# Sparse attention on half of the heads while the other half's queries are projected

## The chip, the cores and the metric

One core of a Trainium2 chip runs the whole network in one launch. The engines are TensorE (PE, with its weight loads as PEld), VectorE (DVE), ScalarE (ACT), GpSimd (POOL) and SyncE (SP), which issues the weight loads. The metric is the device time of one execution in microseconds (us), as the median of several runs; a profile is one execution with a trace.

## The reference, cut to what matters

Two networks of two layers run one after the other on 256 tokens of width 1024. The change lies in the second layer of the first, in its sparse attention (NSA). Every head has three branches; with 256 tokens all blocks are selected, and the window covers all tokens, so two of them are causal attention over 256 keys, each with its own keys and values.

```python
def nsa_mixer(h, kv_cmp, kv_slc, kv_win, w_in, w_out):
    proj = h @ w_in                                  # queries of 16 heads, 48 gates
    ...
    s = einsum(qb, k_cmp) - slope * d_cmp            # 15 compressed keys
    p_cmp = masked_softmax(s, d_cmp >= 0)
    ...
    p_sel = masked_softmax(einsum(qb, k_sel) - slope * d_sel, d_sel >= 0)
    p_win = masked_softmax(einsum(qb, kw) - slope * d_win, m_win)
    o = g[0] * (p_cmp @ v_cmp) + g[1] * (p_sel @ v_sel) + g[2] * (p_win @ vw)
    return o @ w_out
```

The second network has, beside the tokens x, a context of 256 tokens, with its own attention and FFN. Nothing in the first network depends on it; the grouped attention (GQA) of the second network's second layer needs its keys and values.

## The kernel before, in words

**Matrices.** All products are made from float32 weights split into a high and a low part: a weight half of 128x1024 (0.5 MB) is loaded by SP into one of 6 `raw` buffers, ACT casts the high part (L246), DVE subtracts it (L247), and PE makes three matmuls where one would do. Two halves are a slab. In the form that projects to transposed outputs (L492 to L494) a half is 24 matmuls of 128x256; in the other form (L510, L511, L514) the matmuls are 128x512. Split halves have 4 buffers. The slab's instructions have a higher priority, so they are placed early. A scheduler in the recording layer may also move instructions of one engine past each other; what stands on an engine is the program's order, which does not change while it runs.

**Vector steps.** The conditioning vectors of all layers are computed beside the main line: a queue of 0.5 MB loads, each with one or two passes of DVE over 128x1024 (L176). `tick`, called once by each slab, gives credit (the phase's rate, 1.38 unless it has its own), and a step is taken when there is enough. `need` takes steps at once until a vector that is wanted is there. It is called at the head of the output projection for the gate row (`grow`) and for the next FFN's scale and shift (`ab`).

**The context stream.** The context's work is a generator in pieces with an estimated price in us. `fd(us)` runs pieces until the price is used up; a price of 1.3 is 12 matmuls. It is called in the attention loop of NSA, at the boundaries between sublayers and in the second network's first attention; in its first FFN (the stage `bffn0`) every fourth slot takes a piece, and the boundary behind it runs all that is left (`fd(1e9)`) before GQA begins.

**NSA** (stage `a11`, function `nsa`). The gates and the four slabs of queries (8 halves, two heads in each) are projected first. Then the compressed branch is computed for all 16 heads and both token tiles (L816 to L832). Then 16 steps follow, 8 head pairs by 2 token tiles: `stage_a` (scores on PE at L857, bias and maximum on DVE at L865 and L867, exponentials on ACT at L869, sums, L873 to L875), `stage_b` (scaling by sum and gate on DVE at L887, transposes, copy), and after both tiles `stage_c` (values at L904 and L908, split at L484 and L485). `stage_a` runs one step ahead of `stage_b`, and each step calls `fd(1.4)` twice, which takes two pieces of 1.3 each time. The output projection (`proj_gen`, 4 slabs) and the boundary with the residual and the next norm come after.

Of the kernel before, what the change touches and what calls it, by code (L numbers as in the profile page):

```python
# [25 lines left out]
TT = T // P  # L26
# [5 lines left out]
NCMP = 15  # L32
# [38 lines left out]
class Slots:  # L71
# [8 lines left out]
    def next(self):  # L80
        self.i += 1
        return self.parts[(self.i - 1) % len(self.parts)]


class Kern:
# [693 lines left out]
    def nsa(self, h, before_last):  # L779
        nc, I = self.nc, self.I  # L780
        qT = self.chunk().rearrange("p (i t) -> p i t", i=8)
        m0, m1 = self.chunk(), self.r1
        dist = m0[:, 0:512].rearrange("p (t s) -> p t s", t=TT)
        nc.sync.dma_start(dist, I["dist"])
        ctab = m0[:, 512:512 + 480].rearrange("p (t a h n) -> p t a h n", t=TT, a=2, h=8)
        nc.sync.dma_start(ctab, I["ctab"])
        pcT = m0[:, 1024:2048].rearrange("p (g t) -> p g t", g=4)
        gates = m1[:, 544:640].rearrange("p (t b a g r) -> p t b a g r", t=TT, b=3, a=2, g=2)
        cscs = Slots(m1[:, 640:896], 256)
        pcs = Slots(m1[:, 1024:2048], 512)  # L790
        pcl = []
        gw = self.raw_half(I["b_gate"])
        ghi, glo = self.split(gw[:, 0:384], 384)
        hhi, hlo = h
        ps = self.ps([48, T])
# [2 lines left out]
                     kt == 0, kt == KT - 1)  # L798
        gt = self.w([P, T], "htmp", bufs=2)[:48]
        nc.scalar.activation(gt, ps, AF.Tanh, scale=0.5)  # L800
        for s in range(4):
            for half, w in enumerate(self.slab(I["b_w_in"][s])):
                ps = self.ps([P, T])
                self.b_tile(ps, h, w)
                nc.scalar.activation(qT[:, 2 * s + half, :], ps, AF.Copy, scale=0.125)
            if s == 0:
                ps = self.ps([P, TT, 48])
                for t in range(TT):
                    nc.tensor.transpose(ps[:, t, :], gt[:, t * P:(t + 1) * P], self.ident[:48, :48])
                nc.vector.tensor_scalar(m1[:, 544:640], ps.rearrange("p t g -> p (t g)"), 0.5, 0.5, op0=ALU.mult,  # L810
                                        op1=ALU.add)
        for t in range(TT):
            sc = cscs.next()[:, 0:240].rearrange("p (h n) -> p h n", h=16)
            ps = self.ps([P, 8, 2, NCMP])
            for i in range(8):
                nc.tensor.matmul(ps[:, i], qT[:, i, t * P:(t + 1) * P],  # L816
                                 self.kcT[:, i // 4].rearrange("p a n -> p (a n)"), start=True, stop=True)
            for par in range(2):
                nc.vector.tensor_tensor(sc[:, 8 * par:8 * par + 8, :], ps[:, :, par, :], ctab[:, t, par], op=ALU.add)
            mx = self.w([P, 16], "cmx", bufs=2)  # L820
            nc.vector.tensor_reduce(mx, sc, axis=AX.X, op=ALU.max)
            nc.vector.tensor_tensor(sc, sc, mx[:, :, None].to_broadcast([P, 16, NCMP]), op=ALU.subtract)
            nc.scalar.activation(sc, sc, AF.Exp)
            sm = self.w([P, 16], "csm", bufs=2)
            nc.vector.tensor_reduce(sm, sc, axis=AX.X, op=ALU.add)
            nc.vector.tensor_scalar(sm, sm, 1e-30, None, op0=ALU.max)
            nc.vector.reciprocal(sm, sm)
            nc.vector.scalar_tensor_tensor(sm, sm, self.col("valid", t, 1), gates[:, t, 0].rearrange(
                "p a b r -> p (a b r)"), op0=ALU.mult, op1=ALU.mult)
            pc = pcs.next().rearrange("p (h s) -> p h s", h=16)  # L830
            nc.vector.memset(pc, 0.0)
            nc.vector.tensor_tensor(pc[:, :, 0:NCMP], sc, sm[:, :, None].to_broadcast([P, 16, NCMP]), op=ALU.mult)  # L832
            pcl.append(pc)

        def cmp_T():
            for t, pc in enumerate(pcl):
                ps = self.ps([P, 4, P])
                for g in range(4):
                    par, gp = g % 2, g // 2
                    s0 = par * 8 + gp * 4  # L840
                    nc.tensor.transpose(ps[:, g, :], pc[:, s0:s0 + 4, :].rearrange("p a b -> p (a b)"), self.ident)
                nc.scalar.copy(pcT[:, :, t * P:(t + 1) * P], ps)

        hid = self.hid8()
        ca, cb = self.chunk(), self.chunk()
        nps = [Slots(ca[:, 0:512], 256), Slots(ca[:, 512:1536], 512)]
        pts = Slots(cb, 768, 2)
        state = {}

        def stage_a(i, t):  # L850
            gp, r = divmod(i, 4)
            nk = (t + 1) * P
            sps = [self.ps([P, 2, T]) for _ in range(2)]
            for br in range(2):
                for par in range(2):
                    hs = slice(64 * par, 64 * par + 64)
                    nc.tensor.matmul(sps[par][:, br, 0:nk], qT[hs, i, t * P:(t + 1) * P],  # L857
                                     self.kT[br][hs, gp, 0:nk], start=True, stop=True)
            res = []
            mx = self.w([P, 2, 2], "nmx", bufs=4)  # L860
            sm = self.w([P, 2, 2], "nsm", bufs=4)
            for par in range(2):
                slope = 2.0 ** (-8.0 * ((2 * gp + par) * 4 + r + 1) / 16.0)
                p = nps[t].next().rearrange("p (b s) -> p b s", b=2)
                nc.vector.scalar_tensor_tensor(p, dist[:, t, None, 0:nk].to_broadcast([P, 2, nk]),  # L865
                                               -slope, sps[par][:, :, 0:nk], op0=ALU.mult, op1=ALU.add)
# [687 lines left out]
```

## Time and profile before

| | |
|---|---|
| median of 3 runs | 2141.49 us (2139.22 to 2143.03) |
| profiled execution | 2140.95 us, its span 2139.2 us |
| PE, DVE, ACT busy | 94%, 76%, 51% of the span |
| mean granted TensorE clock | 0.979 |
| NSA: first matmul of gates and queries | 917.75 us |
| NSA: first matmul of the compressed branch | 950.2 us |
| NSA: first matmul of the output projection | 1107.8 us |
| last matmul of the main line of `bffn0`, first of GQA | 1802.2 us, 1835.0 us |

Times inside the kernel count from the start of the span. Matmuls are pipelined, so a busy PE can still be slow: a dense stretch is told by the number of matmuls in it. Busy time of DVE is the union of its instructions; their durations can overlap a little.

### The profile page before, as it was taken

To read this page: it belongs to the slowest core of one execution; us is meant where nothing else is said; L and a number is where in the kernel's file an instruction comes from. 1 tells how busy PE (TensorE), PEld (TensorE's weight loads), DVE (VectorE), ACT (ScalarE), POOL (GpSimd) and SP (SyncE) were. 2 spreads that over 40 slices of the span, in tenths; PEclk is the share of its full clock that TensorE was granted. 3 is DMA by queue.
4 is the path that set the end of the run, shared out by engine and by line. 5 is a ranking of instruction groups with operands and counts; after the bars stand their busy time and mean duration, and the time that the engine had idled before them with its cause. 6 is when DMAs were issued, how large, how long until landed. Compare 5 with 4: busy or idle time off the path is not lost. (4 is left out here: it accounts for less than half of the span.)

```text
span 2139.2 us, 34672 instructions
## 1 busy us (share of the span) xinstructions
PE 2013.3 (94%) x13158; PEld 1796.2 (84%) x13158; DVE 1625.5 (76%) x2753; ACT 1087.3 (51%) x1769; POOL 133.6 (6%) x188
## 2 busy tenths in 40 slices
PE   6999899999899899899999999999999998989998
PEld 5998797998789788787788989877789997768998
DVE  7878898777877688878978666789888656866554
ACT  4444545443444466656765444547754444555443
POOL 0000201000200000110000000210010001100000
PEclk9999999999999999989999999999999999999999
DMA  8989697988677766544566866554359755414553
GB/s 332 330 309 355 236 327 277 330 292 291 222 258 276 241 230 210 195 157 138 190 238 232 292 221 237 180 207 148 128 207 342 264 191 178 140 53 150 188 186 118
DMA packets 136327, 486.46 MB, mean 227 GB/s; under 512 B 14976, under 2 KB 16480, under 8 KB 135392
## 3 DMA queue, kind: packets, MB, share of 16 engines
q1 hardware_dynamic: 134240, 477.90, 63.7%
q0 software_dynamic: 1728, 6.29, 0.8%
q8 instruction: 103, 1.69, 0.3%
q14 instruction: 64, 0.52, 0.1%
q10 hardware_dynamic: 192, 0.05, 0.0%
HBM read 480.47 MB, written 3.19 MB: 226 GB/s over the span
## 5 line engine op out<-in xcount | busy, mean ns | idle before, releaser
L1049 ACT ACT_TABLE_LOAD x15 | 19.2, 1283 | 6.6 <-DVE dst.diff0.2984_16079 L1047 1.7
L340 ACT ACT_TABLE_LOAD x13 | 16.7, 1283 | 0.2
L273 PE MATMUL ps.a00.6_101<-ident,x 128*128 128x128 f32 x4 | 1.1, 427 | 13.8 <-DMA x<-in_x 13.8
L375 POOL DMA_DIRECT2D G.bffn0.3378_18457<-row.bffn0.3377_18455 x1 | 0.6, 595 | 198.4 <-DMA row.bffn0.3377_18455<-diag.bffn0.3376_18453 198.4
L273 PEld LDWEIGHTS ps.a00.6_101<-ident,x 128*128 128x128 f32 x4 | 0.7, 216 | 13.7 <-issue 13.7
L375 POOL DMA_DIRECT2D G.a02.1032_5643<-row.a02.1031_5641 x1 | 0.6, 595 | 182.2 <-DMA row.a02.1031_5641<-diag.a02.1030_5639 182.2
L734 ACT ACTIVATE chunk.kv.1231_6595<-chunk.kv.1128_6071,cols 128x60 f32<-128x60 f32 x32 | 9.8, 387 | 4.0 <-PE ps.a10.1253_6672 L744 4.0
L375 POOL DMA_DIRECT2D G.a12.2528_13717<-row.a12.2527_13715 x1 | 0.6, 595 | 180.2 <-DMA row.a12.2527_13715<-diag.a12.2526_13713 180.2
L333 ACT ACT_TABLE_LOAD x9 | 11.5, 1283 | 0.2
L375 POOL DMA_DIRECT2D G.bffn2.3890_21467<-row.bffn2.3889_21465 x1 | 0.6, 595 | 171.6 <-DMA row.bffn2.3889_21465<-diag.bffn2.3888_21463 171.6
L401 POOL TENSOR_TENSOR rv.ctx.354_2048<-ss.ctx.352_2044,epsd 128x1 f32<-128x1 f32 x1 | 0.2, 191 | 169.8 <-ACT junk.ctx.351_2043 L394 169.8
L375 POOL DMA_DIRECT2D G.a11.2165_11615<-row.a11.2164_11613 x1 | 0.5, 530 | 116.9 <-DMA row.a11.2164_11613<-diag.a11.2163_11611 116.9
L484 ACT CAST chunk.a01.490_2583<-chunk.a01.492_2585 128x256 fp32r<-128x256 f32 x8 | 3.2, 406 | 8.9 <-DVE chunk.a01.492_2585 L676 8.9
L287 PE MATMUL ps.a00.38_198<-chunk.a00.20_148,chunk.a00.34_188 128*128 128x256 f32 x8 | 3.2, 401 | 4.8 <-ACT chunk.a00.34_188 L299 2.9
L386 POOL TENSOR_TENSOR rr.ctx.1396_7610<-rv.ctx.1395_7608,nhalf 128x8 f32<-128x8 f32 x1 | 1.6, 1637 | 87.7 <-DVE rv.ctx.1395_7608 L382 87.7
L176 DVE SCALAR_TENSOR_TENSOR vjunk.a12.2456_13210<-raw.a12.2435_13097,srow 128x1024 bf16<-128x1024 f32 x1 | 1.2, 1226 | 7.4 <-DMA raw.a12.2435_13097<-in_ada_w 7.4
L287 PEld LDWEIGHTS ps.a00.38_198<-chunk.a00.20_148,chunk.a00.34_188 128*128 128x128 f32 x8 | 2.0, 254 | 5.7 <-ACT chunk.a00.34_188 L299 3.2
L982 PE MATMUL ps.ctx.1412_7672<-ident,chunk.ctx.453_2431 128*128 128x128 f32 x4 | 1.1, 428 | 5.9 <-DVE chunk.ctx.453_2431 L962 5.9
L869 ACT ACT_TABLE_LOAD x5 | 6.4, 1283 | 0.1
L492 PE MATMUL ps.a10.1241_6626<-chunk.kv.1219_6556,whi.a10.1244_6630 128*128 128x256 f32 x8 | 3.1, 392 | 3.1 <-ACT whi.a10.1244_6630 L246 3.1
L982 PEld LDWEIGHTS ps.ctx.1412_7672<-ident,chunk.ctx.453_2431 128*128 128x128 f32 x4 | 0.7, 218 | 6.3 <-issue 6.3
L386 POOL TENSOR_TENSOR rqc<-rv.ctx.1316_7145,nhalf 128x8 f32<-128x8 f32 x1 | 1.6, 1637 | 62.0 <-DVE rv.ctx.1316_7145 L382 62.0
(11975 smaller groups left out, 9434.4 us busy)
## 6 DMA issues: line engine op xcount, KB each, us to landing
srow<-in_crow SPq DMA_DIRECT2D x3, 512.0 KB, 4.6
x<-in_x SPq DMA_DIRECT2D x1, 1024.0 KB
xc<-in_ctx SPq DMA_DIRECT2D x1, 1024.0 KB
kvd<-chunk.ctx.452_2429 SPq DMA_DIRECT2D x1, 1024.0 KB, 8.3
kvd<-chunk.ctx.451_2428 SPq DMA_DIRECT2D x1, 1024.0 KB
chunk.diff0.2745_14861<-kvd SPq DMA_DIRECT2D x1, 1024.0 KB
chunk.diff0.2746_14862<-kvd SPq DMA_DIRECT2D x1, 1024.0 KB
out<-x SPq DMA_DIRECT2D x2, 512.0 KB, 2.6
```

Of the source, the lines that this page charges most:

```text
L273: nc.tensor.transpose(ps[:, k, t * P:(t + 1) * P], self.x[:, t, kt * P:(kt + 1) * P], self.ident)
L287: mm(out, whi[:, ks], hi[:, k], start=(k == 0), stop=False)
L333: nc.scalar.activation(sg, gate, AF.Silu)
L340: nc.scalar.activation(sg, gate, AF.Silu)
L375: nc.gpsimd.dma_start(G, src.to_broadcast([P, D]))
L386: nc.gpsimd.tensor_tensor(r, v, self.nhalf[:, 0:n], op=ALU.pow)
L484: nc.scalar.copy(hi, src)
L492: mm(out, shi, mhi, start=first, stop=False)
L734: nc.scalar.activation(bt[:, j], self.kv2[i][:, :, 2 * j:2 * j + 16 * (NCMP - 1) + 1:16], AF.Identity, bias=self.col("pos", 16 * i + j, 1))
L869: nc.scalar.activation(p[:, br], p[:, br], AF.Exp, bias=mx[:, par, br:br + 1], accum_out=sm[:, br, par:par + 1])
L982: nc.tensor.transpose(ps[:, j, :], src[:, j * P:(j + 1) * P], self.ident)
L1049: nc.scalar.activation(e[:, :nk], ps[:, :nk], AF.Exp, bias=st[:, m:m + 1], scale=r, accum_out=st[:, 2 + m:3 + m])
```

## The change

Only two of the four query slabs (head pairs 0 to 3) are projected ahead of the attention. The compressed branch is split into two calls, one for each half of the heads, and the first is made at once. The two other slabs become a generator that gives one half at steps 0, 2, 4 and 6. The second call of the compressed branch comes at step 7. `stage_a` runs two steps ahead, with more buffers for its scores. `fd` is called only from step 7 on: 18 times, where there were 33 calls.

```diff
-        for s in range(4):
+        def q_proj(s):
             for half, w in enumerate(self.slab(I["b_w_in"][s])):
                 ps = self.ps([P, T])
                 self.b_tile(ps, h, w)
                 nc.scalar.activation(qT[:, 2 * s + half, :], ps, AF.Copy, scale=0.125)
...
+                yield
+
+        for _ in q_proj(0):
+            pass
...
+        for _ in q_proj(1):
+            pass
+
+        def cmp_p(gp):
+            for t in range(TT):
...
+        def cmp_T(gp):
...
+        cmp_p(0)
         hid = self.hid8()
         ca, cb = self.chunk(), self.chunk()
-        nps = [Slots(ca[:, 0:512], 256), Slots(ca[:, 512:1536], 512)]
+        nps = [Slots([cb[:, 1536:1792], cb[:, 1792:2048], m1[:, 288:544], m1[:, 640:896]]), Slots(ca, 512)]
...
         steps = [(i, t) for i in range(8) for t in range(TT)]
+        def rest():
+            yield from q_proj(2)
+            yield from q_proj(3)
+
+        more = rest()
         stage_a(*steps[0])
-        self.fd(self.nsa_fill)
+        stage_a(*steps[1])
         for n, (i, t) in enumerate(steps):
-            if n + 1 < len(steps):
-                stage_a(*steps[n + 1])
-            self.fd(self.nsa_fill)
+            if n < 8 and n % 2 == 0:
+                next(more)
+            if n == 7:
+                cmp_p(1)
+            if n + 2 < len(steps):
+                stage_a(*steps[n + 2])
+            if n > 6:
+                self.fd(self.nsa_fill)
             stage_b(i, t)
-            self.fd(self.nsa_fill)
-            if n == 1:
-                cmp_T()
+            if n > 6:
+                self.fd(self.nsa_fill)
+            if n in (1, 8):
+                cmp_T(n // 8)
             if t == 1:
                 stage_c(i)
```

Three places in the order of instructions show what moves. On PE, where the attention begins, before: the last matmuls of the eighth query half (ps.a11.1843), then the compressed branch (L816) and the first scores (L857).

```order
L493 MATMUL ps.a11.1843_9879<-chunk.a10.1773_9509,whi.a11.1837_9843 128x256
L494 MATMUL ps.a11.1843_9879<-chunk.a10.1772_9508,wlo.a11.1838_9844 128x256
L816 MATMUL ps.a11.1844_9905<-chunk.kv.1127_6068,chunk.a11.1795_9590 128x30 x7
L816 MATMUL ps.a11.1847_9927<-chunk.kv.1127_6068,chunk.a11.1795_9590 128x30 x7
L857 MATMUL ps.a11.1854_9953<-chunk.kv.1126_6067,chunk.a11.1795_9590 128x128
L857 MATMUL ps.a11.1855_9954<-chunk.kv.1126_6067,chunk.a11.1795_9590 128x128
```

The same place now: the fourth query half (ps.a11.1821) is the last one, the compressed branch is L823, the scores are L866, and a query half (ps.a11.1851) follows the scores of step 1.

```order
L493 MATMUL ps.a11.1821_9741<-chunk.a10.1773_9509,whi.a11.1818_9711 128x256
L494 MATMUL ps.a11.1821_9741<-chunk.a10.1772_9508,wlo.a11.1819_9712 128x256
L823 MATMUL ps.a11.1823_9768<-chunk.kv.1127_6068,chunk.a11.1795_9590 128x30 x3
L823 MATMUL ps.a11.1827_9787<-chunk.kv.1127_6068,chunk.a11.1795_9590 128x30 x3
L866 MATMUL ps.a11.1834_9809<-chunk.kv.1126_6067,chunk.a11.1795_9590 128x128
...
L866 MATMUL ps.a11.1839_9829<-chunk.kv.1126_6067,chunk.a11.1795_9590 128x256
L492 MATMUL ps.a11.1851_9865<-chunk.a10.1772_9508,whi.a11.1843_9849 128x256
```

Four query halves of 24 matmuls have moved from ahead of the compressed branch to between the steps.

On DVE, at the end of the attention, before: vector steps (L176, `vjunk`), the first splits for the output projection (L247, `wlo.a11`) and the split of the last head pair (L485, `chunk.a11`).

```order
L341 TENSOR_TENSOR sg.ctx.2147_11536<-sg.ctx.2147_11536,fps.ctx.2144_11475 128x256
L485 TENSOR_TENSOR chunk.ctx.1974_10489<-sg.ctx.2135_11454,chunk.ctx.1974_10489 128x256
L176 SCALAR_TENSOR_TENSOR vjunk.a11.2197_11722,vec.a11.2176_11635<-raw.a11.2188_11680,srow_78 128x1024
L485 TENSOR_TENSOR chunk.ctx.1974_10489<-sg.ctx.2147_11536,chunk.ctx.1974_10489 128x256
L247 TENSOR_TENSOR wlo.a11.2171_11624<-raw.a11.2169_11621,whi.a11.2170_11623 128x1024
L247 TENSOR_TENSOR wlo.a11.2174_11630<-raw.a11.2172_11627,whi.a11.2173_11629 128x1024
L247 TENSOR_TENSOR wlo.a11.2184_11671<-raw.a11.2182_11668,whi.a11.2183_11670 128x1024
L485 TENSOR_TENSOR chunk.a11.1851_9950<-ps.a11.2160_11594,chunk.a11.1850_9949 128x256
```

The same place now:

```order
L485 TENSOR_TENSOR chunk.a11.1831_9806<-ps.a11.2096_11172,chunk.a11.1830_9805 128x256
L176 SCALAR_TENSOR_TENSOR vjunk.a11.2114_11219,vec.a11.2105_11202<-raw.a11.2111_11213,srow_78 128x1024
L176 SCALAR_TENSOR_TENSOR vjunk.a11.2116_11223,vec.a11.2105_11202<-raw.a11.2113_11217,srow_78 128x1024
L176 SCALAR_TENSOR_TENSOR vjunk.a11.2118_11227,vec.a11.2105_11202<-raw.a11.2115_11221,srow_78 128x1024
L176 SCALAR_TENSOR_TENSOR vjunk.a11.2120_11231,vec.a11.2105_11202<-raw.a11.2117_11225,srow_78 128x1024
L341 TENSOR_TENSOR sg.ctx.2177_11485<-sg.ctx.2177_11485,fps.ctx.2095_11159 128x256
L180 TENSOR_TENSOR vec.a11.2105_11202<-vec.a11.2105_11202,cols 128x8
L176 SCALAR_TENSOR_TENSOR vjunk.a11.2132_11253,vec.a11.2131_11252<-raw.a11.2119_11229,srow_78 128x1024
L247 TENSOR_TENSOR wlo.a11.2126_11241<-raw.a11.2124_11238,whi.a11.2125_11240 128x1024
L247 TENSOR_TENSOR wlo.a11.2129_11247<-raw.a11.2127_11244,whi.a11.2128_11246 128x1024
```

With fewer context slabs in the stage there are fewer ticks, and `need` takes nine vector steps in a row (`vjunk.a11.2103` to `vjunk.a11.2120`); the projection's first split has moved behind them and behind the last head pair.

On PE, behind the main line of `bffn0` (its last matmul is L514 into `ps.bffn0`), before: five more matmuls of the context's FFN, then the transposes of x (L447).

```order
L514 MATMUL ps.bffn0.3078_16551<-whi.bffn0.3413_18652,chunk.bffn0.3374_18450 128x512
L511 MATMUL fps.ctx.3400_18571<-wlo.ctx.3399_18568,chunk.ctx.1974_10489 128x512
L514 MATMUL fps.ctx.3400_18571<-whi.ctx.3398_18567,chunk.ctx.1974_10489 128x512
L510 MATMUL fps.ctx.3401_18572<-whi.ctx.3398_18567,chunk.ctx.1974_10489 128x512
L511 MATMUL fps.ctx.3401_18572<-wlo.ctx.3399_18568,chunk.ctx.1974_10489 128x512
L514 MATMUL fps.ctx.3401_18572<-whi.ctx.3398_18567,chunk.ctx.1974_10489 128x512
L447 MATMUL ps.bffn0.3474_18917<-ident,x 128x128 x2
```

The same place now; "..." stands for the rest of each tile, 11 rows after the first tile and 47 after the next two.

```order
L514 MATMUL ps.bffn0.3031_16166<-whi.bffn0.3360_18239,chunk.bffn0.3329_18045 128x512
L492 MATMUL fps.ctx.3307_17857<-chunk.ctx.2021_10777,whi.ctx.3305_17853 128x256
...
L492 MATMUL fps.ctx.3377_18322<-chunk.ctx.2021_10777,whi.ctx.3372_18312 128x256
...
L492 MATMUL fps.ctx.3385_18388<-chunk.ctx.2021_10777,whi.ctx.3380_18378 128x256
...
L510 MATMUL fps.ctx.3401_18520<-whi.ctx.3396_18510,chunk.ctx.2038_10843 128x512
...
L447 MATMUL ps.bffn0.3486_18955<-ident,x 128x128 x2
```

The context's pieces that NSA no longer takes have moved here: 58 pieces are run in `bffn0` and its boundary, where there were 28; in the stages between the number is as it was (8 and 57).

## Rows read from the trace of the kernel before

**Rows 1.** The page's busy time: us, share of the span, instructions.
```profile
span 2139.2 us, 34672 instructions
PE 2013.3 (94%) x13158; PEld 1796.2 (84%) x13158; DVE 1625.5 (76%) x2753; ACT 1087.3 (51%) x1769; POOL 133.6 (6%) x188
```
**Rows 2.** Busy time by stretch: queries; attention; its output projection; `bffn0`'s boundary.
```profile
core 0: us, PE busy (x) PEld busy (x) DVE busy (x) ACT busy (x) POOL busy (x), PEclk, DMA share, GB/s
917.70:951.00 33.30, 33.00 (x253) 31.06 (x253) 25.58 (x59) 19.27 (x45) 1.65 (x3) 0.96 0.41 139
951.00:1107.80 156.80, 146.02 (x994) 119.06 (x993) 141.71 (x335) 102.45 (x252) 4.99 (x9) 0.96 0.53 178
1107.80:1130.00 22.20, 22.20 (x101) 18.39 (x100) 13.26 (x16) 9.28 (x14) 0.72 (x2) 1.00 0.83 291
1802.50:1835.00 32.50, 24.65 (x107) 18.66 (x105) 23.71 (x40) 17.06 (x36) 5.84 (x12) 0.84 0.28 97
```
**Rows 3.** DVE's L874, once in each of the 16 steps: duration in ns, start.
```profile
L874 DVE RECIPROCAL nsm.a11.1857_9960<-nsm.a11.1857_9960 x1: 172/172/172, 960.7 to 960.7; 128x4 f32<-128x4 f32 x1
...
L874 DVE RECIPROCAL nsm.a11.2134_11430<-nsm.a11.2134_11430 x1: 178/178/178, 1099.0 to 1099.0; 128x4 f32<-128x4 f32 x1
```
**Rows 4.** DVE's waits in the attention (951 to 1108): us in total, times, longest.
```profile
DVE chunk.a11.1851_9950 L485 <- ACT chunk.a11.1850_9949 L484: 4.3, 3, 2.9
DVE wlo.ctx.2103_11239 L247 <- ACT whi.ctx.2102_11238 L246: 1.4, 1, 1.4
DVE csm.a11.1849_9942 L825 <- ACT chunk.kv.1127_6068 L823: 1.2, 1, 1.2
```
**Rows 5.** One query half on PE, its first of three matmuls at each of 8 k.
```profile
L492 PE MATMUL ps.a11.1832_9809<-chunk.a10.1772_9508,whi.a11.1826_9773 x8: 283/283/283, 941.6 to 944.1; 128*128 128x256 f32 x8
```
**Rows 6.** Groups of DVE instructions in the attention: busy us, mean ns, idle before.
```profile
L247 DVE TENSOR_TENSOR wlo.ctx.1977_10493<-raw.ctx.1975_10490,whi.ctx.1976_10492 128x1024 fp32r<-128x1024 f32 x1 | 1.2, 1227 | 0.0
L176 DVE SCALAR_TENSOR_TENSOR vjunk.ctx.2037_10850<-raw.ctx.2019_10730,srow 128x1024 bf16<-128x1024 f32 x1 | 1.2, 1226 | 0.0
L648 DVE TENSOR_TENSOR xc<-xc,fps.ctx.1868_10001 128x512 f32<-128x512 f32 x1 | 0.7, 681 | 0.0
L485 DVE TENSOR_TENSOR chunk.ctx.1974_10489<-sg.ctx.2100_11231,chunk.ctx.1974_10489 128x256 fp32r<-128x256 f32 x1 | 0.4, 426 | 0.0
```
**Rows 7.** DVE's L176, 1080 to 1130: its waits for loads, us, times.
```profile
  DMA raw.a11.2206_11764<-in_ada_w: 1.5, 1
  DMA raw.a11.2175_11633<-in_ada_w: 1.2, 1
  DMA raw.a11.2196_11720<-in_ada_w: 0.9, 1
```
**Rows 8.** The page's DMA rate in 40 slices of the span.
```profile
GB/s 332 330 309 355 236 327 277 330 292 291 222 258 276 241 230 210 195 157 138 190 238 232 292 221 237 180 207 148 128 207 342 264 191 178 140 53 150 188 186 118
```
**Rows 9.** Two stretches of the attention in which PE paused, columns as in Rows 2.
```profile
1000.00:1010.00 10.00, 7.57 (x40) 7.40 (x41) 10.00 (x26) 4.33 (x14) 0.00 (x0) 0.66 0.15 52
1050.00:1060.00 10.00, 6.80 (x37) 4.84 (x35) 9.92 (x20) 4.52 (x13) 0.00 (x0) 0.84 0.54 188
```
**Rows 10.** Pieces of 5 us in `bffn0`'s boundary, columns as in Rows 2.
```profile
1805.00:1810.00 5.00, 3.95 (x22) 3.08 (x20) 4.97 (x8) 2.77 (x7) 2.28 (x5) 1.00 0.05 16
1810.00:1815.00 5.00, 1.02 (x6) 0.42 (x4) 4.56 (x6) 3.29 (x8) 2.27 (x3) 0.96 0.67 229
1815.00:1820.00 5.00, 3.62 (x12) 2.43 (x12) 2.48 (x6) 1.59 (x4) 0.87 (x3) 0.50 0.48 175
1820.00:1825.00 5.00, 4.02 (x11) 3.10 (x12) 4.45 (x12) 2.69 (x7) 0.00 (x0) 0.51 0.00 0
```
**Rows 11.** PE's longest wait, 1050 to 1130: us in total, times, longest.
```profile
PE fps.ctx.2074_11053 L510 <- DVE xc L648: 3.2, 1, 3.2
```
**Rows 12.** Groups of ACT's function-table loads: busy us, mean ns, idle before.
```profile
L340 ACT ACT_TABLE_LOAD x13 | 16.7, 1283 | 0.2
L869 ACT ACT_TABLE_LOAD x5 | 6.4, 1283 | 0.1
```

More of the change, by code (lines that the diff above doesn't have):

```diff
@@ L788, in nsa @@
         gates = m1[:, 544:640].rearrange("p (t b a g r) -> p t b a g r", t=TT, b=3, a=2, g=2)
-        cscs = Slots(m1[:, 640:896], 256)
-        pcs = Slots(m1[:, 1024:2048], 512)
-        pcl = []
+        pcl = [m1[:, 1024 + 512 * t:1536 + 512 * t] for t in range(TT)]
+        for pc in pcl:
+            nc.vector.memset(pc, 0.0)
         gw = self.raw_half(I["b_gate"])
@@ L805, in nsa @@
                 nc.scalar.activation(qT[:, 2 * s + half, :], ps, AF.Copy, scale=0.125)
[L806 to L811, printed above, removed]
-        for t in range(TT):
[L813 to L842, printed above, removed]
+                yield
+        for _ in q_proj(0):
+            pass
+        ps = self.ps([P, TT, 48])
@@ new lines, in nsa @@
+        for t in range(TT):
+            nc.tensor.transpose(ps[:, t, :], gt[:, t * P:(t + 1) * P], self.ident[:48, :48])
+        nc.vector.tensor_scalar(m1[:, 544:640], ps.rearrange("p t g -> p (t g)"), 0.5, 0.5, op0=ALU.mult, op1=ALU.add)
+        for _ in q_proj(1):
+            pass
+        def cmp_p(gp):
+            for t in range(TT):
+                scf = self.w([P, 256], "misc", bufs=1)[:, 0:8 * NCMP]
+                sc = scf.rearrange("p (h n) -> p h n", h=8)
+                ps = self.ps([P, 4, 2, NCMP])
+                for i in range(4):
+                    nc.tensor.matmul(ps[:, i], qT[:, 4 * gp + i, t * P:(t + 1) * P],
+                                     self.kcT[:, gp].rearrange("p a n -> p (a n)"), start=True, stop=True)
+                for par in range(2):
+                    nc.vector.tensor_tensor(sc[:, 4 * par:4 * par + 4, :], ps[:, :, par, :],
+                                            ctab[:, t, par, 4 * gp:4 * gp + 4], op=ALU.add)
+                mx = self.w([P, 8], "cmx", bufs=2)
+                nc.vector.tensor_reduce(mx, sc, axis=AX.X, op=ALU.max)
+                nc.vector.tensor_tensor(sc, sc, mx[:, :, None].to_broadcast([P, 8, NCMP]), op=ALU.subtract)
+                nc.scalar.activation(scf, scf, AF.Exp)
+                sm = self.w([P, 8], "csm", bufs=2)
+                nc.vector.tensor_reduce(sm, sc, axis=AX.X, op=ALU.add)
+                nc.vector.tensor_scalar(sm, sm, 1e-30, None, op0=ALU.max)
+                nc.vector.reciprocal(sm, sm)
+                nc.vector.scalar_tensor_tensor(sm.rearrange("p (a r) -> p a r", a=2), sm.rearrange("p (a r) -> p a r", a=2),
+                                               self.col("valid", t, 1), gates[:, t, 0, :, gp, :],
+                                               op0=ALU.mult, op1=ALU.mult)
+                for par in range(2):
+                    pc = pcl[t].rearrange("p (h s) -> p h s", h=16)[:, 8 * par + 4 * gp:8 * par + 4 * gp + 4, 0:NCMP]
+                    nc.vector.tensor_tensor(pc, sc[:, 4 * par:4 * par + 4, :],
+                                            sm[:, 4 * par:4 * par + 4, None].to_broadcast([P, 4, NCMP]), op=ALU.mult)
@@ L844, in nsa @@
+        def cmp_T(gp):
+            for t in range(TT):
+                ps = self.ps([P, 2, P])
+                for par in range(2):
+                    s0 = 32 * (par * 8 + gp * 4)
+                    nc.tensor.transpose(ps[:, par, :], pcl[t][:, s0:s0 + P], self.ident)
+                nc.scalar.copy(pcT[:, 2 * gp:2 * gp + 2, t * P:(t + 1) * P], ps)
+        cmp_p(0)
         hid = self.hid8()
         ca, cb = self.chunk(), self.chunk()
-        nps = [Slots(ca[:, 0:512], 256), Slots(ca[:, 512:1536], 512)]
+        nps = [Slots([cb[:, 1536:1792], cb[:, 1792:2048], m1[:, 288:544], m1[:, 640:896]]), Slots(ca, 512)]
```

## The prediction

> **What bounds the kernel now.** I read the busy times first: PE 94% of the span, DVE 76%, ACT 51% [rows 1]. The share of PE says little by itself, so the stages came next, by windows around NSA and around the place where the context's work ends. The reader is to compare the number of matmuls. While queries are projected, PE does 253 in 33.3 us, with DVE busy for 25.6 of them. In the attention it does 994 in 156.8, fewer in each microsecond although it counts as busy for 146, while DVE is busy for 141.7; the output projection is dense again, and DVE has 13.3 of 22.2 [rows 2]. So PE sets the pace before and behind the attention, and in the attention, I take it, DVE does. The steps support that: L874 stands once in each, the first at 960.7 and the last at 1099.0, 138.3/15 = 9.2 us a step, and DVE's busy time is 141.7/16 = 8.9 us a step [rows 2, 3]. DVE's waits there are short, the longest entry 4.3 us in three pieces, all in all 156.8 - 141.7 = 15.1 us of idle time [rows 2, 4].
>
> The sum is made against the profiled execution, 2140.95 us with a span of 2139.2, that is 1.8 us around it; it lies 0.5 us under the median of 2141.49.
>
> **Query halves between the steps.** Four halves of 24 matmuls leave the stretch that PE sets. A half's first matmuls at each k run from 941.6 to 944.1, seven distances of three matmuls, 0.12 us each [rows 5]; 4 x 24 x 0.12 = 11.5 us. The order shows the compressed branch right behind the fourth half. So the attention starts 11.5 us earlier. The halves now stand on PE between scores, in a stretch where PE has room: it would be 994 matmuls less 294 of the context (below) plus 96. Their splits on DVE do not enter the attention, since the order keeps them ahead of it, in the free DVE time of the queries' stretch. If the cover is gone, these 11.5 us stay on the path.
>
> **Context pieces leave the attention.** 18 calls instead of 33. Counted in the order from the first scores to the last head pair, PE loses 228 matmuls of 128x256 and 66 of 128x512. On PE that is 228 x 0.12 = 27.4 and 66 x 0.22 = 14.5 us (22.2 us for 101 in the projection [rows 2]), 41.9 us. But DVE is what counts here, so I counted its order from the compressed branch to the first matmul of the output projection, everything that must be done before PE can go on. Splits: 30 before, three of them for the projection itself; 18 now, two for the projection; 12 less at 1.22 us, -14.6. Vector steps: 22 and 23, +1.2. The context's residual updates (L645, L648) 16 and 8, at 0.68, -5.4; its gate products and splits (L341, L485) 16 and 6, at 0.42, -4.2 [rows 6]. The second call of the compressed branch, a tail of the context's attention that moves in from just before, and small instructions +3. Sum: -20 us. DVE's idle time bounds it: if two steps of lead remove all its waits, 15 us more are gained; if the first seven steps, without fill, wait for exponentials as they come, I would lose some 10 of it. I take -20, with the share of idle time as it is, because that is what the row shows.
>
> **Vector steps in a row.** `need` takes nine at the head of the output projection, and with those of the last slabs eleven loads of 0.5 MB stand on SP ahead of the projection's first weights, where before they were mixed with slabs. DVE's part is in the count above: in the order the projection's first split now stands behind them, where before three splits were done before the last head pair. The loads are not. 13 loads (eleven and the two of the first slab) are 6.8 MB; at the projection's 291 GB/s [rows 2] 23 us, at the span's best slice, 355 [rows 8], 19 us. DVE has about 22 us of work beside them (an estimate: 13 vector steps at 1.22 and five splits and small ones). Even before, DVE waits 1.5, 1.2 and 0.9 us for such loads [rows 7]. Bounds 0 and +10; I take +3. PE has little queued behind the last head pair and idles there; where it paused in the attention its clock fell to 0.66 and 0.84 of full over 10 us [rows 9], at half rate 7 and 3 us long, a loss of 3.4 and 1.6 us in a dense stretch. The dense projection follows, so +2, bounds 0 and +4.
>
> **Pieces run later.** The 30 pieces that NSA drops are not lost: the stages between take as many as before, so they all arrive at the boundary behind `bffn0`, which must finish the context before GQA. There they stand by themselves. DVE was busy for 23.7 of 32.5 us there and gets little new, so PE sets their pace: +41.9 us. Between output blocks PE waits for DVE's residual update, 3.2 us in one case [rows 11]; three more such places, partly filled by x's transposes, +5 (0 to +10). Against this PE has gaps while x's own norm is made, 1.0 and 4.0 us in the two pieces from 1805 to 1815 [rows 10], which the new pieces can fill, -4 (0 to -12, if the half-clock time from 1815 to 1825 goes too). The chain of the context's last norm and its keys cannot be hidden, since it comes behind the last piece. Sum +43, bounds +30 to +52.
>
> **Free or nearly so.** The scores two steps ahead take more buffers, which lie in free parts of tiles; the clearing of the compressed probabilities moves ahead of the gates, under PE's query matmuls.
>
> **The sum.** -11.5 - 20 + 3 + 2 + 43 = +16.5 us; 2141.0 + 16.5 = 2157.5 us. Work that ran beside a DVE-bound stretch and shared it is put where it runs alone; in the stretch it costs DVE's time, 20 us, and in its new place PE's, 43.
>
> **A rule on table loads.** ACT changes its function table 11 times in NSA's attention (all five of L869, and six of L340's 13) because the context's silu stands between exponentials; in the order one is left. Each takes 1.28 us [rows 12], ten are 12.8 us. ACT is busy for 102 of 156.8 us [rows 2], so I price them at nothing. The Trainium skill, "ScalarE: Activation LUTs", section "What ACT_TABLE_LOAD costs", speaks for more: a switch of set costs the load of 1.28 us, which this trace confirms, and a drain of about as much, 2.66 us together, and its rules tell to group calls by set. By it ten loads would be 27 us, and the sum 2131.
>
> **Rivals.**
> PE, not DVE, sets the attention's pace: for it, PE's busy time, 146.0, is even above DVE's 141.7, and DVE's scores wait on PE behind fill matmuls, which two steps of lead would end. Then the stretch shrinks by what PE loses, 41.9 - 11.5 = 30.4, instead of by 20, and with the 11.5 ahead of it the gain is 41.9. The pieces then go where they cost the same, and with no DVE burst to wait for at the projection (its +3 and +2 fall away) and the gaps at the boundary filled to their bound, 30 instead of 43, the sum is -41.9 + 30 = -12, 2129 us. It decides from the point where a step with fill falls under 8.5 us. Against it: 994 matmuls in 156.8 us, while 253 took 33.3.
> The table loads were on the path: the gain is 12.8 us larger, 2157.5 - 12.8 = 2144.7. Against it: ACT is idle for a third of the stretch.
> The loads in a row hit in full, and the seven steps without fill wait for ACT: +10 for +3, +4 for +2, and a gain of 16 for 20; 2157.5 + 13 = 2170.5. For it: waits for such loads exist already.
> The change doesn't keep the context out of the first half: the order shows 24 of its matmuls before step 8's values. That moves nothing between stages, and has the forecast's time.
>
> **How the numbers follow.** Forecast 0.66, with a range of its own of 2149 to 2167; PE sets the pace 0.10; table loads 0.09; loads in full 0.15. About 0.2%, 4.3 us, is what a measurement of this kernel can tell from no change. Faster: the first rival but for its upper end, 0.09. Same: the table loads, that upper end and the low tail of the forecast, 0.12. Slower: the rest, 0.79. The range for 8 in 10 leaves out the first rival below and half of the third above: 2138 to 2173.
>
> **What would show it.** Right: the output projection's first matmul at about 1081 (1107.8 less 31.5, plus 5), behind a run of L176 on DVE; steps with fill still some 9 us apart, those without about 5 to 6; GQA's first matmul about 75 us behind the last of `bffn0`'s main line, where it was 32.7; PE dense in the first 50 of them. Wrong: steps with fill under 8.5 us, or the projection before 1070 (the gain is larger); a boundary under 62 us (the pieces found gaps).

## The result and the profile after

The changed kernel takes 2165.2 us (4 runs, 2151.7 to 2167.3) where the kernel before takes 2140.4 in the same series; ratio 1.0103, 95% interval 1.0059 to 1.0147. A later series gave 1.0092 (1.0062 to 1.0123). The forecast was 2157.5 us, 1.0077 of the profiled execution. The profiled execution took 2164.3 us:

```profile
span 2162.5 us, 34710 instructions
PE 2024.9 (94%) x13158; PEld 1809.5 (84%) x13158; DVE 1627.1 (75%) x2775; ACT 1073.8 (50%) x1761; POOL 137.9 (6%) x188
```

Beside [rows 1] these shares say nothing: 23 us more, and PE still at 94% with as many matmuls. The stages, cut at the starts of matmuls, say where (us, up to the last matmul, 6.6 us ahead of the span's end; the second execution is the profiled one of the later series, 2152.1 us):

| stage | before | after | after, second | forecast of the difference |
|---|---|---|---|---|
| all ahead of NSA, unchanged | 917.8 | 924.7 | 915.6 | 0 |
| gates and queries ahead of the attention | 32.4 | 21.0 | 20.9 | -11.5 |
| compressed branch to the last values | 157.3 | 123.1 | 123.1 | -20 |
| last values to the output projection | 0.3 | 8.0 | 7.6 | +3 |
| output projection | 21.7 | 23.8 | 24.1 | +2 |
| NSA's boundary | 16.7 | 14.3 | 14.3 | 0 |
| the FFN behind NSA | 206.1 | 209.7 | 206.6 | 0 |
| `bffn0`'s boundary | 32.7 | 83.5 | 81.9 | +43 |
| all other stages behind it | 747.6 | 747.8 | 749.6 | 0 |

The forecast's -20 counts DVE's work up to the projection's first matmul, so it is fairly held against the two rows of the attention and the pause together: -17 forecast with the +3, -26.5 and -26.9 measured.

Windows of the changed kernel on the queries, the attention to its last values, the pause, the two together, the projection and `bffn0`'s boundary (columns as in [rows 2], which they answer):

```profile
924.70:945.70 21.00, 20.71 (x151) 18.82 (x150) 18.18 (x49) 13.20 (x36) 1.64 (x3) 0.94 0.25 91
945.70:1068.80 123.10, 115.73 (x801) 91.60 (x800) 111.13 (x311) 77.09 (x227) 5.56 (x9) 0.94 0.40 136
1068.80:1076.80 8.00, 4.87 (x41) 4.37 (x37) 7.76 (x16) 2.00 (x5) 0.53 (x1) 1.00 1.00 371
945.70:1076.80 131.10, 120.59 (x838) 95.97 (x837) 118.89 (x326) 79.09 (x232) 6.09 (x10) 0.95 0.44 150
1076.80:1100.60 23.80, 23.27 (x95) 18.86 (x96) 19.74 (x24) 11.31 (x14) 0.18 (x1) 0.93 1.01 377
1774.90:1858.40 83.50, 70.15 (x414) 60.90 (x412) 50.99 (x73) 36.38 (x64) 6.62 (x12) 0.92 0.38 135
```

The reader is to subtract PE's busy time from each length. To the last values PE idles 123.1 - 115.7 = 7.4 us; the same window of the kernel before gives

```profile
950.20:1107.80 157.60, 146.82 (x1002) 119.86 (x1000) 141.95 (x335) 103.18 (x252) 4.99 (x9) 0.96 0.53 179
```

that is 10.8 us of 157.6. In the pause of 8 us DVE is busy for 7.76. Its timeline there (start, length) has vector steps back to back, and none of them waits for its load:

```profile
1070.07 1.21 DVE L176 SCALAR_TENSOR_TENSOR vjunk.a11.2114_11219<-raw.a11.2111_11213,srow 128x1024 bf16<-128x1024 f32 x1
...
1071.33 1.23 DVE L176 SCALAR_TENSOR_TENSOR vjunk.a11.2116_11223<-raw.a11.2113_11217,srow 128x1024 bf16<-128x1024 f32 x1
...
1072.59 1.23 DVE L176 SCALAR_TENSOR_TENSOR vjunk.a11.2118_11227<-raw.a11.2115_11221,srow 128x1024 bf16<-128x1024 f32 x1
```

PE, however, does wait for a load there. Its first matmul of the projection needs ACT's cast of the first weight half, `raw.a11.2124`. That half can only be loaded when one of the 6 `raw` buffers is free, and the rows follow each other within hundredths of a us: a vector step on DVE ends with the read of its sum at 1069.82, SP issues the load at 1069.84, the load lands after 5.84 us, the cast takes 1.04, and the matmul starts at 1076.8.

```profile
1068.59 1.22 DVE L176 SCALAR_TENSOR_TENSOR vjunk.a11.2112_11215<-raw.a11.2109_11209,srow 128x1024 bf16<-128x1024 f32 x1
1069.74 0.08 DVE L176 DVE_READ_ACCUMULATOR vjunk.a11.2112_11215<-raw.a11.2109_11209,srow 128x1 f32 x1
1069.84 0.33 SPq L237 DMA_DIRECT2D raw.a11.2124_11238<-in_b_w_out  x1
1075.70 1.04 ACT L246 CAST whi.a11.2125_11240<-raw.a11.2124_11238 128x1024 fp32r<-128x1024 f32 x1 [1.62 <-DMA raw.a11.2124_11238<-in_b_w_out]
PE ps.a11.2122_11236 L510 <- ACT whi.a11.2125_11240 L246: 3.1, 1, 3.1
```

The attention's steps are shorter than forecast. L883 is the L874 of [rows 3]; the tenth and the last one start at

```profile
L883 DVE RECIPROCAL nsm.a11.1922_10308<-nsm.a11.1922_10308 x1: 167/167/167, 1003.5 to 1003.5; 128x4 f32<-128x4 f32 x1
...
L883 DVE RECIPROCAL nsm.a11.2054_10885<-nsm.a11.2054_10885 x1: 169/169/169, 1045.8 to 1045.8; 128x4 f32<-128x4 f32 x1
```

which is 42.3/6 = 7.1 us a step in the half that carries the context, where the forecast had some 9 and named 8.5 as the point below which PE sets the pace. In `bffn0`'s boundary PE is busy throughout only in the first 20 us (50 were forecast); then it pauses, and its granted clock falls to 0.83 and 0.69 in two of the stretches. PE's waits name the residual update L648, as [rows 11] did in the attention, and the gate product L341:

```profile
1775.00:1785.00 10.00, 10.00 (x85) 9.96 (x84) 9.29 (x12) 7.32 (x16) 4.17 (x6) 1.00 0.51 170
1785.00:1795.00 10.00, 10.00 (x81) 9.78 (x81) 4.89 (x7) 5.08 (x8) 0.00 (x0) 1.00 0.68 232
1795.00:1805.00 10.00, 9.35 (x51) 7.69 (x50) 6.73 (x9) 2.79 (x5) 0.00 (x0) 1.00 0.43 153
1805.00:1815.00 10.00, 7.93 (x41) 7.08 (x40) 4.75 (x6) 2.31 (x3) 0.00 (x0) 0.83 0.40 149
...
1825.00:1835.00 10.00, 5.57 (x23) 3.97 (x24) 6.82 (x11) 3.37 (x6) 0.19 (x1) 1.00 0.21 75
1835.00:1845.00 10.00, 4.96 (x21) 3.30 (x20) 6.37 (x14) 4.83 (x13) 2.27 (x5) 0.69 0.29 105
```
```profile
PE fps.ctx.3417_18604 L492 <- DVE xc L648: 2.1, 1, 2.1
PE fps.ctx.3434_18737 L510 <- DVE sg.ctx.3426_18719 L341: 2.0, 1, 2.0
PE fps.ctx.3447_18793 L447 <- DVE xc L648: 1.8, 1, 1.8
```

### The profile page after: what moved, and what is told of

Same layout as the page of the kernel before. It is cut to its first block, busy times and chain, and to the rows that moved or that the text cites. A ratio compares the mean times of both kernels' runs of the same rounds, so it can differ in the third digit from the quotient of the medians.

```text
span 2162.5 us, 34710 instructions
## 1 busy us (share of the span) xinstructions
PE 2024.9 (94%) x13158; PEld 1809.5 (84%) x13158; DVE 1627.1 (75%) x2775; ACT 1073.8 (50%) x1761; POOL 137.9 (6%) x188
## 4 chain that ended last, share of the span: by engine, by line
PE 65%; DVE 14%; DMA 9%; issue 5%; ACT 4%; POOL 3%; SPq 0%; DVEq 0%; POOLq 0%; ACTq 0%
PE ps.a10.1253_6672 L744 1%; DVE x L640 0%; DMA x<-in_x 0%; DMA raw.ctx.359_2061<-in_ada_w 0%; DMA raw.a02.1070_5840<-in_ada_w 0%; PE ps.a10.1291_6979 L744 0%; DMA raw.a02.924_4991<-in_ada_w 0%; DMA raw.a12.2364_12539<-in_ada_w 0%; DMA raw.a02.984_5352<-in_ada_w 0%; DMA raw.bffn0.3134_16715<-in_ada_w 0%; DMA raw.bffn0.3053_16254<-in_ada_w 0%; DVE xc L648 0%; DMA raw.a10.1438_7784<-in_ada_w 0%; DMA raw.a10.1648_8933<-in_ada_w 0%; DMA raw.a02.1005_5467<-in_ada_w 0%
## 5 line engine op out<-in xcount | busy, mean ns | idle before, releaser
L333 ACT ACT_TABLE_LOAD x9 | 11.5, 1283 | 0.2
L995 DVE TENSOR_TENSOR chunk.diff0.2572_13786<-chunk.diff0.2572_13786,chunk.diff0.2571_13785 128x512 f32<-128x512 f32 x8 | 5.5, 682 | 0.0
```

The source lines that it names most:

```text
L333: nc.scalar.activation(sg, gate, AF.Silu)
L995: nc.vector.tensor_tensor(o, o, o2, op=ALU.add)
```

## Experiments

Each row under an experiment is a window of its trace, columns as before. Four experiments (more work for DVE, more for PE, less for DVE in either kernel) were executed once each, with the trace, so they are read by their stretches and not by their totals. How well these repeat: kernels that are alike there take 131.1, 130.7 and 130.1 us from the compressed branch to the projection (123.1, 123.1 and 121.2 to the last values) in the changed form, and 157.6 and 157.4 in the form before.

**The context in all steps again.**

```diff
         stage_a(*steps[0])
+        self.fd(self.nsa_fill)
...
-            if n > 6:
-                self.fd(self.nsa_fill)
+            self.fd(self.nsa_fill)
...
```

> The changed kernel with the context's calls in all 16 steps, as before the change; the queries between the steps, the split compressed branch and the scores two steps ahead stay. Theory (in the attention DVE's time sets the pace, and work moved out of it costs PE's full time where it lands): the queries' 11.5 us are saved, the attention is as long as before, 157.6 us from its compressed branch to the projection (152 to 160, if the second step of lead removes a few waits), no vector steps stand in a row, the boundary behind bffn0 is back at 33 us: 2129 us (2122 to 2134). Rival A (PE sets the attention's pace): the queries only change place, the attention grows by 11.5 to 169 us, 2140 us (2137 to 2143). Rival B (the lead of two steps is what made the attention shorter): it removes the 15 us of DVE's idle time, the attention takes 142 us, 2114 us.

Measured: 2140.6 us, ratio 0.9964 (0.9945 to 0.9982), 6.5 us faster than before (2147.1 in this series). The boundary is 33.1 us, the pause 0.3.

```profile
949.60:1110.90 161.30, 152.79 (x1098) 127.43 (x1096) 150.12 (x366) 109.45 (x264) 5.41 (x9) 0.99 0.60 196
```

From the compressed branch to the projection it is 3.6 us longer than before, between theory (0) and rival A (11.5). PE idles 8.5 us of it and DVE 11.2. So queries and lead are a small gain, and the loss of the change lies in the context's restriction.

**The restriction alone**, in the kernel before.

```diff
-        self.fd(self.nsa_fill)
...
-            self.fd(self.nsa_fill)
+            if n > 6:
+                self.fd(self.nsa_fill)
...
```

> The kernel before with one thing changed: the context's calls only from step 7 on. Queries all ahead, scores one step ahead, as before. Theory: DVE loses 20 us in the attention, 3 to 8 are given back in the vector steps in a row ahead of the projection, the boundary behind bffn0 is 83 us as in the changed kernel: 2140 - 20 + 5 + 51 = 2176 us (2170 to 2184). Rival A (PE sets the attention's pace): PE loses 41.9 us there, so the attention shrinks by some 40 and the loss is 10: 2150 us. Rival B (without the second step of lead the steps without context wait for exponentials and scores): the attention shrinks by 10 or less, 2186 us.

Measured: 2181.7 us, ratio 1.0148 (1.0129 to 1.0168), boundary 83.7 us.

```profile
963.10:1095.50 132.40, 111.26 (x706) 85.64 (x704) 110.47 (x292) 76.09 (x219) 6.03 (x9) 0.87 0.40 135
963.10:1020.00 56.90, 45.28 (x269) 32.82 (x268) 47.98 (x140) 31.13 (x104) 0.88 (x2) 0.84 0.34 117
1020.00:1095.50 75.50, 65.98 (x437) 52.82 (x437) 62.49 (x153) 44.96 (x115) 5.15 (x8) 0.89 0.45 149
```

The total is near the theory's, but for other reasons: the attention lost 25.2 us, and in it PE now idles 21.1 us at a mean clock of 0.87. With one step of lead and less context to fill in, the steps wait, as rival B said, and not only the first ones: 11.6 us of PE's idle time lie in the first 57 us, 9.5 in the 75 behind. Rival B's size, 10 us or less off the attention, failed. To the last values the changed kernel needs 123.1 with 11.5 us of queries in it, this one 132.1. So the lead and the queries together are worth most where the context has left; they differ at once between the two kernels, and no run shows what either gives alone.

**17 us more for DVE in the changed kernel.**

```diff
-                nc.vector.tensor_reduce(mx[:, par, :], p, ...
+                for _ in range(2):
+                    nc.vector.tensor_reduce(mx[:, par, :], p, ...
```

> The changed kernel with each step's two maximum reductions on DVE (L876) done twice: 32 more instructions, 16 of 0.41 us and 16 of 0.67, 17.3 us of DVE's time and nothing of PE's. Theory (DVE sets the attention's pace): from the compressed branch to the projection's first matmul 131.1 us become 146 to 150. Rival A (PE sets it): 131 to 137. If both share it by waiting for each other: 138 to 145.

Measured: 150.1 us, the upper end of the theory's range; 136.5 to the last values and a pause of 13.7.

```profile
942.60:1092.60 150.00, 123.48 (x838) 97.13 (x837) 133.75 (x358) 82.47 (x234) 6.03 (x10) 0.92 0.40 135
```

**20 us more for PE in the changed kernel.**

```diff
-                for par in range(2):
+                for par in (0, 1, 0, 1, 0, 1):
```

> The changed kernel with each score matmul (L866) done three times into the same place: two more sets in each of 16 steps, a set of 0.43 us where a step has 128 keys and 0.86 where it has 256, 20.6 us of PE's time and nothing of DVE's. Theory (DVE sets the attention's pace): from the compressed branch to the projection's first matmul 131.1 us become 131 to 138. Rival A (PE sets it): 148 to 152. If both share it by waiting for each other: 139 to 147.

Measured: 144.8 us, "shared" by the list. To the last values 144.4, 21.3 more, which is all of the added work (to the projection 13.7 more); the pause is 0.3, 7.7 less.

```profile
945.00:1089.70 144.70, 132.53 (x1058) 107.77 (x1058) 121.78 (x324) 78.79 (x229) 4.35 (x9) 1.00 0.41 137
```

Read together: in the changed kernel DVE sets the way to the projection, some 8 us behind the last values, and work for PE first eats those 8 us. On the way to the last values PE's added work counts in full, but 13.3 of DVE's 17.3 us count there too: neither engine has room to spare. The added matmuls stand ahead of a step's softmax, so this run does not tell PE's time apart from the length of a step's chain.

**The changed kernel once more**, unedited, for the next two.

> The changed kernel once more, beside the two variants of it below on the same chip. The two full tables of stages differ in places that the change does not touch (the stage ahead of NSA 6.9 us longer, the feed-forward behind it 3.6 us), with more low clock there. Theory (those are the clock of single executions): the loss against before is the sum of the touched stages, -38 + 2 - 2 + 51 = +13 us, ratio 1.004 to 1.010, and the stage ahead of NSA as long as before. Rival (the change causes them, by a transfer or a step that comes earlier): +23 us and the same stages longer again.

Measured: 2162.8 us (7 runs, 2152.1 to 2168.2), ratio 1.0092. The touched stages repeat within 2 us, and the stage ahead of NSA is 915.6, so its 924.7 was that of one execution. The ratio lies in the theory's range; its +13 is too small for the medians (+21) all the same, and the profiled execution happened to be the fastest of the seven.

**Vector steps moved to the first steps.**

```diff
+            for _ in range(2 if n < 2 else n < 7):
+                self.step()
```

> The changed kernel with nine vector steps (L176) issued one by one in the first seven steps, two in each of the first two, so that none stands in a row at the projection's head. In the first 54 us of the attention DVE is busy for 46.7 and PE for 51.5. Theory (PE and DVE are both near their limit; the row costs its wait, and DVE's 11 us find 7 us of idle time in the first half): the projection starts 0.3 us behind the last values instead of 8.0 and takes 21.7 us instead of 23.8, the last values come 2 to 6 us later; together 3 to 7 us faster than the changed kernel. Rival A (DVE's time is the same wherever it stands): from the compressed branch to the projection still 131 us, 0 to 2 faster. Rival B (it was the loads in a row alone): last values as before, 10 us faster.

Measured: 2177.5 us, 14.7 slower than the changed kernel beside it. All three expectations failed on the total; the stretch alone is near rival A:

```profile
946.60:1081.30 134.70, 120.45 (x802) 94.69 (x800) 118.26 (x325) 80.48 (x230) 6.41 (x9) 0.92 0.50 163
```

The pause is 0.3 and the last values come 11.3 us later, DVE's nine steps in full (9 x 1.22 = 11.0): the first half had no room for DVE's work. What the rest of the 14.7 us is, scattered over queries, projection and FFN, stays open.

**The boundary's pieces in the main line.**

```diff
- 'run_d': 4,
+ 'run_d': 1,
```

> The changed kernel in which bffn0's main line takes a context piece at every place it has (run_d 1 for 4), so that 4 pieces are left for its boundary instead of 45. In the main line PE is busy for 207.7 of 209.7 us. Theory (a piece costs PE's full time wherever PE is dense, and alone it costs the waits between pieces too): the 41 pieces lengthen the main line by about 47 us (57.7 of the boundary's 83.5 before its last chain, less 9 to 10 of waits), the boundary is 25 to 35 us: 5 to 15 us faster than the changed kernel. Rival (the pieces find room beside the feed-forward, and only standing alone is dear): main line up by 10 or less, 40 us faster.

Measured: 2138.9 us, ratio 0.9977 (0.9953 to 1.0001): the whole loss is gone. Main line and boundary:

```profile
1563.00:1829.80 266.80, 263.87 (x1795) 245.65 (x1796) 187.20 (x243) 120.38 (x153) 3.05 (x7) 0.99 0.68 235
1829.80:1839.70 9.90, 7.93 (x47) 6.79 (x46) 9.40 (x17) 7.70 (x18) 5.77 (x8) 1.00 0.46 143
```

The main line grew by 57.1 us, 1.39 a piece, so the pieces find no room there; the boundary shrank by 73.6. Together they are 16.5 us shorter, a little above the theory's 5 to 15, since the boundary is 9.9 us and not 25 to 35. The medians are 23.9 us apart (2162.8 and 2138.9); the 7 us beyond these two stages are not placed by a trace.

**7 us less for DVE in the kernel before.**

```diff
-                nc.vector.tensor_reduce(mx[:, par, :], p, ...
+                nc.vector.tensor_reduce(mx[:, par, :], p[:, :, ::4], ...
```

> The kernel before with the maximum in each step's softmax (L867) taken over every fourth key, which shifts the exponent and leaves the quotient what it is: 32 reductions of 0.41 and 0.67 us, 17.3 us of DVE's time, become 4 to 9 us, 8 to 13 less, and nothing of PE's changes. Theory of the prediction (DVE alone sets the attention's pace in the kernel before): 157.6 us become 145 to 149. Rival A (PE sets it): 154 to 158. If the two are bound to each other: 150 to 153.

Measured: 157.1 us for 157.6. The reductions take 0.26 and 0.37 us, 7.2 us less in all, a little under the 8 to 13 expected. DVE is busy for 135.8 where it was 141.95, and nothing is gained. PE is busy for 1.2 us longer in this execution; without these it would be 155.9, still rival A's. So DVE did not set the pace, nor did its part of a step's chain, from which the time was taken. ACT is busy for 107 of the 157 us, and PE is what remains; no run took PE's work alone away.

```profile
958.90:1116.00 157.10, 148.03 (x1001) 119.76 (x1000) 135.80 (x336) 106.71 (x254) 4.61 (x9) 0.95 0.55 182
```

**The same in the changed kernel.**

> The changed kernel with the maximum in each step's softmax (L876) taken over every fourth key: 32 reductions, 7.2 us of DVE's time less (measured in the kernel before: 0.26 and 0.37 us for 0.41 and 0.67), nothing of PE's. PE and DVE are both at about 92% here to the last values. Theory (PE sets the way to the last values, 123.1 us; the 8 us behind it are DVE's arrears, nine vector steps with no wait for a load between them): last values at 120 to 123 us, the gap ahead of the projection 1 to 5 us. Rival A (the loads in a row set the gap): the gap stays 7 to 9. Rival B (DVE sets the whole stretch): the last values 6 to 7 us earlier, at 116 to 117.

Measured: last values after 121.2 us, within what the unedited kernel shows (121.2 to 123.1), and a pause of 2.8, as the theory said; to the projection 124.0 for 130.1 to 131.1, so 6.1 to 7.1 of DVE's 7.2 us.

```profile
947.80:1068.90 121.10, 116.09 (x800) 90.52 (x800) 107.92 (x317) 75.87 (x227) 5.17 (x9) 0.97 0.46 153
1068.90:1071.70 2.80, 2.80 (x25) 2.46 (x22) 2.72 (x7) 1.57 (x3) 0.00 (x0) 1.00 1.02 338
```

The projection's first load is issued 117.7 us behind the first matmul of the compressed branch, for 124.2 in the first trace of the changed kernel, and lands after 5.0 us; ACT's cast waits for it here too, for 0.6 us. That one execution still took 2163.6 us, with 926.8 us ahead of NSA and 214.4 in the FFN behind it.

**Drain in the main line, in the kernel before.** The edit is that of `run_d`.

> The kernel before with the drain of the previous run alone: bffn0's main line takes a context piece at every place (run_d 1 for 4), and none is left for its boundary. In the changed kernel with that drain the main line and the boundary took 276.7 us with 58 pieces, 1.39 us a piece in the main line (57.1 / 41); with 28 pieces 276.7 - 30 x 1.39 = 235 us, where they are 243.4 now. Theory: boundary 10 us, together 8 us faster than before. Rival (the last chain of the context's keys is waited for wherever it stands): 0 to 2 us faster.

Measured: 2137.5 us, ratio 0.9955 (0.9939 to 0.9971), 8.9 us faster; main line and boundary 236.6 us for 243.4, 6.7 less (243.39 and 236.64):

```profile
1596.60:1825.00 228.40, 225.52 (x1537) 208.24 (x1538) 163.17 (x216) 104.54 (x135) 7.63 (x9) 1.00 0.70 241
1825.00:1833.20 8.20, 3.32 (x22) 2.46 (x20) 5.63 (x8) 4.65 (x13) 2.98 (x6) 0.79 0.50 167
```

Of the 16.5 us that this edit gave in the changed kernel, 9.8 are thus what the pieces that came there by the change cost beyond their time in the main line.

**That drain with the first experiment's kernel.**

> The context in all steps (as in the first run), queries between the steps, scores two ahead, and bffn0's main line taking a context piece at every place. Theory: the first run's gain (7.7 us) and that of the previous kernel (8 us) add up: 16 us faster than before, ratio 0.991 to 0.994. Rival (what two steps of lead give is what the drain gives, both being idle time of PE in the same executions): no faster than the better of the two, 0.996.

Measured: 2127.2 us, ratio 0.9917 (0.9892 to 0.9942), 19.1 us faster: the two gains (6.5 and 8.9) add up within the interval.

**And the maximum over every fourth key.**

> The previous kernel with the maximum over every fourth key, 7.2 us of DVE's time less in the attention. In the first run PE was busy for 152.4 and DVE for 149.7 of the attention's 160.9 us. Theory (PE sets the pace): 0 to 3 us faster than the previous kernel. Rival (DVE sets it): 7 us faster.

Measured: 2124.3 us, ratio 0.9899 (0.9879 to 0.9919), the fastest version; 2.9 us under the previous kernel, whose interval it overlaps. The attention is 157.9 us for 162.1 (161.2 in the first run), PE idle for 3.8 of them; the 3.3 to 4.2 us lie between theory and rival, so with two steps of lead and the queries inside a part of DVE's time is on the path here:

```profile
938.60:1096.50 157.90, 154.13 (x1096) 127.73 (x1094) 142.61 (x367) 109.10 (x264) 6.51 (x9) 0.99 0.62 200
```

## Why the forecast was right, and where it was not

The direction and the place were right: work that ran beside other work in NSA came back by itself in `bffn0`'s boundary and cost more there. The closeness of the total is in part luck: the attention came out 9.5 us better than forecast, the boundary 8 us worse, and 10 to 12 us of the medians' difference lie in no term of the sum. The forecast's own marks met it halfway: the projection begins at 1076.8 (forecast 1081), the boundary is 83.5 us (about 75), and the steps with fill are 7.1 us apart, which it had named as a sign of being wrong.

**Query halves**: -11.5 forecast, -11.5 measured (32.44 to 20.97).

**Context pieces leave the attention**: this step failed. It said that DVE sets the attention's pace and gave -20; measured is -34.2 to the last values, and -26.5 to the projection with the pause in it. With 7 us of DVE's time taken out of the kernel before, the attention stays as long as it is. The rival "PE sets the pace" fits: PE loses 41.9 us of context, gains 11.5 of queries, and idles 3.4 less (10.8 to 7.4), together 33.8 of the 34.2; this is an account, not an experiment. The forecast read "fewer matmuls in each microsecond" as room on PE, but a count mixes widths: some 160 of those in [rows 2] have 512 columns and start 0.23 us apart (the median), not a query's 0.12; the 10.8 us in which no matmul ran were the better measure there. The Trainium skill, "Perfetto Trace Analysis", section "Identifying the Most-Contended Engine", says that TensorE's matmul busy share does not show well how close it is to its roofline, and tells to judge it by the share of peak FLOPs used and by the busy share of weight loads, and VectorE by its occupancy. The weight loads are busy for 120 of 157.6 us here and DVE for 142, which names DVE too (the share of peak was not worked out); the run with less work for DVE decides against it.

DVE was close behind, however, and to the projection the changed kernel goes at DVE's pace: 7.2 us less of it gave 6.1 to 7.1, 17.3 more cost 19.0 to 20.0. The count of -20 was near what DVE lost (23.1 us of busy time, 141.95 to 118.89; the trace has 24 and 23 vector steps where the count had 22 and 23). It was the sum of a path that was not the longest in the kernel before and became so by the change.

**Vector steps in a row**: +3 and +2 for the clock; measured +7.7 and +2.1, with -2.4 in NSA's boundary. The place was right and the +3 too small, nearer to the third rival's +10. The sum took the loads as a queue that runs beside DVE's work. In the trace a load waits until a vector step frees a buffer (the five issued from 1065.6 to 1071.3 follow the end of a vector step within 0.03 us), so the time at which the projection's first load is issued follows DVE's work; that is why the pause shrinks with it. Behind it the load's 5.8 us and the cast's 1.0 stand in full (7.9 us for the load where DVE had more work, 5.0 where it had less). Spreading the steps over the first part of the attention moved the cost there.

**Pieces run later**: +43, measured +50.8 and +49.2 (with the main line ahead of it +49.8 in both). PE's 41.9 us for 30 pieces hold, since a piece costs 1.39 us in a dense line (41.7). The 9 us on top of them (9.8 by the two runs with the drain moved) are the mis-sized term: waits of 5 were taken, and -4 for gaps that would be filled, but PE's idle time rose from 8 to 13.4 us, and its busy time by 45.5. That is also why the rival's total of 2129 failed, though its account of the attention held: it had the boundary at 30, and no pause.

The touched stages sum to +12.5 and +10.7 in the two executions (forecast +16.5). The medians are 21 to 25 us apart. The table loads fell in the attention from 11 to 1 as said, but PE's account of the stretch closes to 0.4 us without them; no run took them away alone.

**Open**: the 10 to 12 us between the stages' sum and the medians. The FFN behind NSA takes 206.6 to 216.1 us in every trace of a kernel with the late context, and 203.1 to 206.1 in the others; why is not settled. The rest goes with the granted clock of whole runs (below), and no trace shows where the unprofiled runs lose their time.

## What to carry to other kernels

Where two engines are both busy for 90% of a stretch, settle which one sets the pace by taking a few microseconds of work away from one. A count of instructions does not tell it, and idle time does not do so safely: in the kernel before it named the right engine (PE idle for 10.8 us, DVE for 15.7), on the changed kernel's way to the projection it would have named the wrong one (PE 10.5, DVE 12.2). Where weights are loaded into a few buffers, an engine that frees them late delays the next load, and the load's whole time can stand behind it. Work that is moved from a stage with a bound to a place where it stands alone brings its whole time and its waits; in the main line of a dense stage it brought its time alone, and 10 us of waits less. What a deeper lead, queries between the steps and a lighter filling are worth depends on each other, so they are to be tried apart; the lead and the queries were not.

## What the runs showed of the hardware

Run time went with the mean granted clock in each kernel: in the later series the kernel before took 2133.1 us at 0.980 and 2153.7 at 0.971, the changed kernel 2152.1 at 0.973 and 2168.2 at 0.966. A straight line through all runs gives 1.5 us (16 runs) and 2.1 us (7 runs) for each 0.001. The medians, 0.977 and 0.969, differ by 0.008, which at these rates goes with 12 to 17 of the 21 us between the kernels. With the drain in the main line the runs are back at 0.974 to 0.980. This does not make the clock the cause: its mean also falls where the change itself makes PE pause, and the 12 to 17 us overlap with the stages' sum. At the same mean of 0.971 the kernel before took 2149.6 to 2153.7 us and the changed one 2161.3. In the traces the clock falls after pauses of PE: in `bffn0`'s boundary the share is 1.00 from 1825 to 1835, with PE busy for 5.6 of these 10 us, and 0.69 in the next 10, the last 5 of them at 0.50, which is the lower of its two levels, 1.2 GHz.
